# Taking the causal mask of the row maxima from TensorE to VectorE, and putting the first memory-attention units ahead of the last projections

## The chip, the cores and the metric

The kernel runs on one core of a Trainium2 chip, as one program. The metric is the device time of one execution in microseconds (us). TensorE (PE in the profile, with its weight loads as PEld), VectorE (DVE), ScalarE (ACT) and GpSimd (POOL) each run their own queue of instructions in order; SyncE (SP) issues most transfers.

## The reference, cut to what matters

Two decoder layers over 2,048 positions of width 1,024. Each has 12 heads of causal softmax attention (layer 0 with low-rank projections and a rotary part, layer 1 with a forget-gate bias) and 4 heads of attention over 256 memory tokens, fed by one combined input projection and followed by gating, an output projection and a norm.

```python
def causal_block_attention(q, k, v, scale, log_f_cum=None):
    ...
        s = jnp.einsum('bqhd,bkhd->bhqk', q_i, k, preferred_element_type=jnp.float32) * scale
        if log_f_cum is not None:
            s = s + (args[2][..., None].astype(jnp.float32) - f_t[:, :, None, :].astype(jnp.float32))
        q_pos = i * BLOCK_Q + jnp.arange(BLOCK_Q)
        mask = key_pos[None, :] <= q_pos[:, None]
        s = jnp.where(mask, s, -jnp.inf)
        p = jax.nn.softmax(s, axis=-1)
        return jnp.einsum('bhqk,bkhd->bqhd', p.astype(v.dtype), v)

def memory_attention(q, k, v):
    s = jnp.einsum('bshd,bmhd->bhsm', q, k, preferred_element_type=jnp.float32) * (MEM_DIM ** -0.5)
    p = jax.nn.softmax(s, axis=-1)
    return jnp.einsum('bhsm,bmhd->bshd', p.astype(v.dtype), v)
```

## The kernel before, in words

The program goes through input projection, attention and output projection of layer 0, then the same of layer 1. A number of full precision is held as a high and a low part, so that a product takes two or three matmuls.

Attention is cut into **units**: one head and one group `g` of 512 queries. A causal unit has four query tiles of 128. For each tile the **maxima** are found first: query rows against keys in chunks of up to 512 columns (L1578), each into one bank of a ring of three PSUM banks (`ap["pm"]`), and VectorE reduces each chunk to one column (L1544). The last chunk of each tile is the **diagonal** one, 128, 256, 384 or 512 columns wide; its last 128 columns need the causal mask. TensorE puts it there: a matmul of the identity `idb` with the mask `mqk` (L1577) starts the bank, and the matmul of queries and keys adds to it. A unit with `g > 0` has `g + 1` chunks a tile, gathered in `mx` and reduced once more by `nm` (L1589); a unit with `g = 0` has one chunk a tile and writes the negated maximum straight to `nmw`. A small matmul then turns the four columns into a row (L1596), which VectorE writes under the queries (L1597), so that the **logits** (L1705, transposed, with a mask of their own at L1667 and L1671) come out with the maximum subtracted. ScalarE takes the exponential (L1647) and its high part (L201), GpSimd or VectorE the low part (L223), and TensorE multiplies with the **values** (L1721). A head has 4 units and 16 diagonal chunks; 24 heads have 384.

The order on all engines is written out by `run_units` under `manual_schedule`: while the logits of one unit run, the maxima of units up to `AHEAD = 5` further on are put between them. A memory unit has no mask; its maxima are at L1555.

Ahead of that, `att_start` runs the first memory units of a layer (6 in layer 0, 8 in layer 1) by `run_early`, while the last projections (L254, from `proj_b` in layer 1 and from `up_a` in layer 0) still run. Here a list scheduler sets the order by priorities, which follow the order in which the code records instructions; `high_priority(offset=n)` moves what it encloses ahead by n.

Of the kernel before, what the change touches and what calls it, by code (L numbers as in the profile page):

```python
# [10 lines left out]
F32 = mybir.dt.float32  # L11
# [10 lines left out]
P = 128  # L22
# [28 lines left out]
PV_AHEAD = 120  # L51
MEM_EARLY = {0: 6, 1: 8}
# [139 lines left out]
class Trunk:  # L192
# [64 lines left out]
    def constants(self, ctx):  # L257
# [17 lines left out]
        self.mqk = cp.tile([P, P], BF16, name="mqk")  # L275
        nc.gpsimd.memset(self.mqk, 0.0)
        nc.gpsimd.affine_select(out=self.mqk, in_=self.mqk, compare_op=ALU.is_ge, fill=NEG, base=0,
                                pattern=[[-1, P]], channel_multiplier=1)
# [738 lines left out]
    def att_start(self, l):  # L1017
# [27 lines left out]
        run_early(mem, first)  # L1045
# [30 lines left out]
    def attention(self):  # L1076
# [6 lines left out]
        gb, fewer = B("G"), None  # L1083
        more = (v0, yb, gb, ap["sp"]) if l == 0 else (ap["ymp"], gb, v0, v0)
# [401 lines left out]
class Unit:  # L1486
# [46 lines left out]
    def max_closures(self):  # L1533
# [11 lines left out]
        if not self.causal:  # L1545
# [13 lines left out]
            self.nchunk = 1  # L1559
            return out  # L1560
        self.nchunk = g + 1
        for t in range(4):
            nk = (4 * g + t + 1) * P
            for c in range(self.nchunk):

                def f(t=t, nk=nk, c=c):
                    (q, qr), (k, kr) = self.mx_ops
                    if t == 0 and c == 0:
                        start()
                        if self.nchunk > 1:  # L1570
                            self.mx = K.sm.tile([P, 4, NG], F32, name="mx", tag="mx", bufs=AHEAD + 2)
                    x = c * G
                    w = min(G, nk - x)
                    ps = ap["pm"].tile([P, w], F32, name="pm", tag="pm")
                    diag = x + w == nk
                    if diag:
                        nc.tensor.matmul(ps[:, w - P:w], lhsT=K.idb, rhs=K.mqk, start=True, stop=False, skip_group_check=True)  # L1577
                    nc.tensor.matmul(ps, lhsT=q[0:qr, t * P:(t + 1) * P], rhs=k[0:kr, x:x + w],  # L1578
                                     start=not diag, stop=True, skip_group_check=diag)
                    if self.nchunk == 1:  # L1580
                        reduce(self.nmv[:, t:t + 1], ps, True)
                    else:
                        reduce(self.mx[:, t, c:c + 1], ps, False)
                out.append((f, min(G, nk - c * G)))
        return out

    def nm(self):
        if self.nchunk > 1:
            self.K.nc.vector.tensor_reduce(out=self.nmv, in_=self.mx[:, :, 0:self.nchunk], axis=AX.X, op=ALU.max, negate=True)  # L1589
# [201 lines left out]
```

## Time and profile before

| | |
|---|---|
| median of 3 runs | 2927.8 us (2927.29 to 2934.29) |
| the profiled execution | 2922.26 us, span of its instructions 2920.2 us |
| granted TensorE clock, mean | 0.975 |
| busy over the span | PE 2822.9 us, PEld 2394.5, DVE 1556.6, ACT 1324.8, POOL 1249.0 |
| attention of layer 0 and of layer 1 | about 650 to 1290 us, 2170 to 2705 us |

Busy time is the time in which an engine has an instruction running. Matmuls are pipelined, and the ends that the profile gives them are modelled, so what one costs is read from start to start, not from its own duration. PEclk is the granted clock as a share of full speed: 1.00 stands for 2.4 GHz, 0.50 for 1.2 GHz.

### The profile page before, as it was taken

To read this page: it belongs to the slowest core of one execution; us is meant where nothing else is said; L and a number is where in the kernel's file an instruction comes from. 1 tells how busy PE (TensorE), PEld (TensorE's weight loads), DVE (VectorE), ACT (ScalarE), POOL (GpSimd) and SP (SyncE) were. 2 spreads that over 40 slices of the span, in tenths; PEclk is the share of its full clock that TensorE was granted. 3 is DMA by queue.
4 is the path that set the end of the run, shared out by engine and by line. 5 is a ranking of instruction groups with operands and counts; after the bars stand their busy time and mean duration, and the time that the engine had idled before them with its cause. 6 is when DMAs were issued, how large, how long until landed. Compare 5 with 4: busy or idle time off the path is not lost. (4 is left out here: it accounts for less than half of the span.)

```text
span 2920.2 us, 58773 instructions
## 1 busy us (share of the span) xinstructions
PE 2822.9 (97%) x24401; PEld 2394.5 (82%) x24401; DVE 1556.6 (53%) x2950; ACT 1324.8 (45%) x1867; POOL 1249.0 (43%) x836
## 2 busy tenths in 40 slices
PE   7999999879999999999999999999999999999998
PEld 6789998657788888878888988999767788787787
DVE  6522115567676777645463345310267687777343
ACT  5321123336777777752131010111137788888311
POOL 2110114336667777772201014200037778788421
PEclk9999999979999999999999999999979999999999
DMA  5333447763433334245443226831454444364453
GB/s 191 123 134 95 126 144 266 234 200 91 98 75 85 77 90 97 57 162 194 150 153 128 75 67 209 311 127 62 130 148 112 116 130 122 109 163 161 153 178 116
DMA packets 260931, 398.43 MB, mean 136 GB/s; under 512 B 24792, under 2 KB 140520, under 8 KB 260520
## 3 DMA queue, kind: packets, MB, share of 16 engines
q1 hardware_dynamic: 180112, 255.21, 30.8%
q10 hardware_dynamic: 79016, 138.27, 13.1%
q8 instruction: 192, 3.15, 0.5%
q0 software_dynamic: 1536, 1.18, 0.3%
q14 instruction: 75, 0.61, 0.1%
HBM read 238.13 MB, written 156.47 MB: 135 GB/s over the span
## 5 line engine op out<-in xcount | busy, mean ns | idle before, releaser
L223 POOL TENSOR_TENSOR bA<-bA,bA 128x1024 f16<-128x1024 f32 (+5 forms) x277 | 507.0, 1841 | 311.1 <-ACT bA L201 223.8
L1544 DVE TENSOR_REDUCE mx<-banks 128x1 f32<-128x512 f32 (+2 forms) x864 | 511.9, 618 | 194.2 <-PE banks L1578 188.4
L254 PE MATMUL banks<-bR,bA 128*128 128x256 f32 (+3 forms) x4437 | 551.4, 286 | 0.6 <-DVE bQ L510 0.6
L254 PEld LDWEIGHTS banks<-bR,bA 128*128 128x128 f32 x4437 | 542.9, 189 | 5.4 <-DVE bQ L510 0.8
L254 PE MATMUL banks<-bA,bR 128*128 128x512 f32 (+2 forms) x2208 | 510.1, 388 | 6.5 <-ACT bS L823 3.6
L1705 PE MATMUL banks<-bA,bA 96*128 96x512 f32 (+13 forms) x1820 | 484.1, 377 | 0.9 <-ACT bA L1647 0.8
L254 PEld LDWEIGHTS banks<-bA,bR 128*128 128x128 f32 x2208 | 401.2, 190 | 91.9 <-ACT bS L823 4.1
L1647 ACT ACTIVATE bA<-banks 128x1024 f32<-128x1024 f32 (+1 forms) x414 | 370.9, 896 | 201.2 <-PE banks L1705 177.3
L201 ACT ACTIVATE bA<-bA 128x1024 f16<-128x1024 f32 (+5 forms) x400 | 336.4, 848 | 95.1 <-DMA qrs<-bA 20.6
L1705 PEld LDWEIGHTS banks<-bA,bA 96*128 96x128 f32 (+3 forms) x1820 | 327.7, 193 | 43.4 <-ACT bA L1647 1.7
L1578 PE MATMUL banks<-bA,bA 76*128 76x512 f32 (+5 forms) x868 | 335.4, 424 | 10.0 <-DMA bA<-qbs 4.6
L208 POOL TENSOR_SCALAR bR<-bR 128x1024 fp32r<-128x1024 f32 (+3 forms) x50 | 61.6, 1231 | 403.9 <-PE banks L254 349.0
L1222 PE MATMUL banks<-bA,bA 128*128 128x512 f32 x960 | 227.5, 393 | 0.0
L1721 PEld LDWEIGHTS <-bA 128*128 128x128 f16 x5928 | 198.0, 99 | 29.7 <-issue 12.1
L1222 PEld LDWEIGHTS banks<-bA,bA 128*128 128x128 f32 x960 | 179.3, 189 | 36.3
L1705 PE MATMUL banks<-bR,bA 128*128 128x512 f32 (+6 forms) x620 | 202.3, 393 | 0.6 <-DVE bR L1597 0.3
L223 POOL TENSOR_TENSOR bR<-bR,bR 128x1024 f16<-128x1024 f32 (+2 forms) x74 | 160.0, 2162 | 89.6 <-ACT bR L201 48.0
L1193 POOL TENSOR_TENSOR bA<-bA 128x512 f32<-128x512 f32 x64 | 101.8, 1613 | 208.7 <-DMA bA<-gs 196.7
L1578 PEld LDWEIGHTS banks<-bA,bA 76*128 76x128 f32 (+1 forms) x868 | 167.4, 200 | 24.2 <-issue 9.9
L223 POOL TENSOR_TENSOR bR<-bA,bR 128x1024 f16<-128x1024 f32 (+2 forms) x76 | 154.7, 2037 | 74.1 <-ACT bR L201 28.2
L508 ACT ACTIVATE bG<-banks 128x256 f32<-128x256 f32 x128 | 49.1, 385 | 285.6 <-PE banks L254 229.2
L223 DVE TENSOR_TENSOR bR<-bR,bR 128x1024 fp32r<-128x1024 f32 (+5 forms) x66 | 79.7, 1211 | 185.6 <-POOL bR L208 169.7
(228 smaller groups left out, 3697.8 us busy)
## 6 DMA issues: line engine op xcount, KB each, us to landing
bA<-qbs SPq DMA_DIRECT2D x65, 256.0 KB
bA<-in_x_dram SPq DMA_DIRECT2D x32, 512.0 KB
gs<-bG ACTq DMA_DIRECT2D x128, 128.0 KB
bA<-gs SPq DMA_DIRECT2D x32, 512.0 KB
bA<-ys SPq DMA_DIRECT2D x32, 512.0 KB
bA<-h SPq DMA_DIRECT2D x28, 512.0 KB
ks<-bA ACTq DMA_DIRECT2D x24, 512.0 KB
qs<-bA ACTq DMA_DIRECT2D x24, 512.0 KB
```

The source lines that it names most:

```text
L201: nc.scalar.activation(out, in_, AF.Copy, scale=scale)
L208: nc.gpsimd.tensor_scalar(out, in_, scale, 0.0, op0=ALU.mult, op1=ALU.add)
L223: e.tensor_tensor(out=out, in0=in_, in1=hi, op=ALU.subtract)
L254: nc.tensor.matmul(out, lhsT=a, rhs=b, start=start and i == 0, stop=stop and i == n - 1)
L508: nc.scalar.activation(st[:, 0:2 * P], ps[:, 0:2 * P], AF.Silu)
L1193: nc.gpsimd.tensor_tensor(out=gt[:, hs], in0=gt[:, hs], in1=yt[:, hs], op=ALU.mult)
L1222: nc.tensor.matmul(ps[:, ns], lhsT=a, rhs=b[:, ns], start=c == 0 and j == 0, stop=c == KC - 1 and j == 2)
L1544: nc.vector.tensor_reduce(out=to, in_=ps, axis=AX.X, op=ALU.max, negate=negate)
L1578: nc.tensor.matmul(ps, lhsT=q[0:qr, t * P:(t + 1) * P], rhs=k[0:kr, x:x + w], start=not diag, stop=True, skip_group_check=diag)
L1647: nc.scalar.activation(pf[:, 0:w], ps[:, 0:w], AF.Exp, scale=self.scale, bias=LOGP)
L1705: nc.tensor.matmul(ps[:, o:o + bw], lhsT=k[0:kr, (self.k0 + kt) * P:(self.k0 + kt + 1) * P], rhs=q[0:qr, q0:q0 + bw], start=i == 0 and not ...
L1721: nc.tensor.matmul(self.pv[:, t, 0:n], lhsT=p[:, o:o + P], rhs=v[:, kv, a:a + n], start=self.first, stop=False, skip_group_check=True)
```

## The change

The mask of the maxima leaves TensorE. `tensor_tensor_reduce` on VectorE takes the bank and the mask, adds them, writes the sum to a scratch tile `mj` and the maximum to `mx`. The mask tile is now 512 wide, zero but for its last 128 columns, and made on GpSimd at the start of each layer's attention. A unit with `g = 0` goes by `mx` and `nm` like the others. Beside it, `run_early` is enclosed in a priority offset of 1500.

```diff
+EARLY_AHEAD = 1500
...
-        self.mqk = cp.tile([P, P], BF16, name="mqk")
-        nc.gpsimd.memset(self.mqk, 0.0)
-        nc.gpsimd.affine_select(out=self.mqk, in_=self.mqk, compare_op=ALU.is_ge, fill=NEG, base=0,
-                                pattern=[[-1, P]], channel_multiplier=1)
...
-        run_early(mem, first)
+        with self.tc.high_priority(offset=EARLY_AHEAD):
+            run_early(mem, first)
...
+        mb, jb = (v0, yb) if l == 0 else (ap["sp"],) * 2
+        mqk = self.mqk = mb.tile([P, G], BF16, name="mqk")
+        ap["mj"] = Turn(jb.tile([P, G], BF16, name="mj"))
+        nc.gpsimd.memset(mqk, 0.0)
+        nc.gpsimd.affine_select(out=mqk[:, G - P:G], in_=mqk[:, G - P:G], compare_op=ALU.is_ge, fill=NEG, base=0,
+                                pattern=[[-1, P]], channel_multiplier=1)
...
-                    diag = x + w == nk
-                    if diag:
-                        nc.tensor.matmul(ps[:, w - P:w], lhsT=K.idb, rhs=K.mqk, start=True, stop=False, skip_group_check=True)
-                    nc.tensor.matmul(ps, lhsT=q[0:qr, t * P:(t + 1) * P], rhs=k[0:kr, x:x + w],
-                                     start=not diag, stop=True, skip_group_check=diag)
-                    if self.nchunk == 1:
-                        reduce(self.nmv[:, t:t + 1], ps, True)
+                    nc.tensor.matmul(ps, lhsT=q[0:qr, t * P:(t + 1) * P], rhs=k[0:kr, x:x + w], start=True, stop=True)
+                    to = self.mx[:, t, c:c + 1]
+                    if x + w == nk:
+                        nc.vector.tensor_tensor_reduce(out=ap["mj"].next()[:, 0:w], in0=ps, in1=K.mqk[:, G - w:G], scale=1.0,
+                                                       scalar=-3.0e38, op0=ALU.add, op1=ALU.max, accum_out=to)
                     else:
-                        reduce(self.mx[:, t, c:c + 1], ps, False)
+                        reduce(to, ps, False)
...
     def nm(self):
-        if self.nchunk > 1:
-            self.K.nc.vector.tensor_reduce(out=self.nmv, in_=self.mx[:, :, 0:self.nchunk], axis=AX.X, op=ALU.max, negate=True)
+        if not self.causal:
+            return
+        self.K.nc.vector.tensor_reduce(out=self.nmv, in_=self.mx[:, :, 0:self.nchunk], axis=AX.X, op=ALU.max, negate=True)
```

The first causal unit of layer 0 on TensorE, before: four masks, each with a weight load of its own, and the four diagonal chunks behind them, ahead of the row matmul.

```order
L1577 LDWEIGHTS idb
L1577 MATMUL banks<-mqk,idb 128x128
L1578 MATMUL banks<-bA_5120,bA_5290 128x128
L1577 LDWEIGHTS idb
L1577 MATMUL banks<-mqk,idb 128x128
L1578 MATMUL banks<-bA_5120,bA_5290 128x256
L1577 LDWEIGHTS idb
L1577 MATMUL banks<-mqk,idb 128x128
L1578 MATMUL banks<-bA_5120,bA_5290 128x384
```

The same place on TensorE in the changed kernel, where the chunks have line 1577 and the row matmul line 1597:

```order
L1597 MATMUL banks<-idr,nmw 68x128
L1577 MATMUL banks<-bA_5115,bA_5289 128x128
L1577 MATMUL banks<-bA_5115,bA_5289 128x256
L1577 MATMUL banks<-bA_5115,bA_5289 128x384
L1577 MATMUL banks<-bA_5115,bA_5289 128x512
L1597 MATMUL banks<-idr,nmw 68x128
```

The masks and their weight loads are gone, 384 of each in the program; nothing else on TensorE has moved here. On VectorE the same unit was four reduces in a row, between two writes of rows under queries:

```order
L1597 TENSOR_TENSOR bA_4690<-banks,spread 4x512
L1544 TENSOR_REDUCE nmw<-banks 128x1 x4
L1597 TENSOR_TENSOR bA_4690<-banks,spread 4x512
L1544 TENSOR_REDUCE mx<-banks 128x1 x3
L1597 TENSOR_TENSOR bA_5290<-banks,spread 4x512
```

In the changed kernel (`bA_5267` holds the scratch tile, `bA_5114` the mask):

```order
L1580 ISA bA_5267,mx<-banks,bA_5114 128x128
L1580 ISA mx 128x1
L1580 ISA bA_5267,mx<-banks,bA_5114 128x256
L1580 ISA mx 128x1
L1580 ISA bA_5267,mx<-banks,bA_5114 128x384
L1580 ISA mx 128x1
L1580 ISA bA_5267,mx<-banks,bA_5114 128x512
L1580 ISA mx 128x1
L1598 TENSOR_TENSOR bA_4685<-banks,spread 4x512
L1590 TENSOR_REDUCE nmw<-mx 128x4
```

Each diagonal chunk is now two instructions, the sum with its maximum and a second one that writes the [128, 1] result; behind the four stands one more reduce. The program has 768 such instructions in place of 384 reduces, and 96 reduces at `nm` in place of 72.

TensorE at the end of the projections of layer 1, before: the last nine projection matmuls (L254), with maxima and logits of memory units around them.

```order
L1555 MATMUL banks<-bA_21294,bR_21298 128x256 x2
L1705 MATMUL banks<-bA_21294 128x512 x2
L254 MATMUL banks<-bA_14744,bR_16184 128x512
L254 MATMUL banks<-bA_14745,bR_16184 128x512
L254 MATMUL banks<-bA_14744,bR_16185 128x512
L1555 MATMUL banks<-bA_21294 128x256 x2
L1705 MATMUL banks<-bR_21298,bA_21294 128x512
L1596 MATMUL banks<-idr,nmw 68x128
```

In the changed kernel (projections at L255, maxima of memory units at L1559, logits at L1706):

```order
L1559 MATMUL banks<-bA_21125,bR_21129 128x256 x2
L1706 MATMUL banks<-bR_21129,bA_21125 128x512 x2
L255 MATMUL banks<-bA_14575,bR_16016 128x512
L255 MATMUL banks<-bA_14575,bR_16015 128x512
L255 MATMUL banks<-bA_14576,bR_16015 128x512
L255 MATMUL banks<-bA_14575,bR_16016 128x512
L1559 MATMUL banks<-bA_21125 128x256 x2
L1706 MATMUL banks<-bR_21129,bA_21125 128x512
L1597 MATMUL banks<-idr,nmw 68x128
```

The rows read alike but belong to the unit after: 239 projection matmuls stand behind the first memory unit's first maxima, where there were 192, and the values of six of the eight early units stand ahead of the last projection, where there were five. In layer 0 the order of the early units among the projections is the same, row by row, on all engines.

## Rows read from the trace of the kernel before

**Rows 1.** The page, busy time, share of the span and instructions of each engine.
```profile
PE 2822.9 (97%) x24401; PEld 2394.5 (82%) x24401; DVE 1556.6 (53%) x2950; ACT 1324.8 (45%) x1867; POOL 1249.0 (43%) x836
```
**Rows 2.** Busy time by stretch: start:end, length, busy us (instructions) of each engine, PEclk, DMA.
```profile
876.00:949.00 73.00, 72.98 (x878) 59.69 (x874) 50.85 (x91) 57.06 (x72) 54.26 (x31) 1.00 0.34 85
...
2409.00:2482.00 73.00, 72.70 (x1000) 59.15 (x996) 57.52 (x103) 63.18 (x72) 60.28 (x29) 1.00 0.47 121
```
**Rows 3.** Groups by line: count, busy us, mean ns, idle before and what ended it.
```profile
L1544 DVE TENSOR_REDUCE mx<-banks 128x1 f32<-128x512 f32 (+2 forms) x864 | 511.9, 618 | 194.2 <-PE banks L1578 188.4
...
L1577 PE MATMUL banks<-mqk,idb 128*128 128x128 bf16 x384 | 88.8, 233 | 1.1 <-DVE mx L1544 0.5
...
L1596 PE MATMUL banks<-idr,nmw 128*68 128x128 f32 (+1 forms) x128 | 32.2, 251 | 7.0 <-DVE nmw L1544 5.6 <-DVE bA L1597 1.1 <-DVE nmw L1589 0.3
```
**Rows 4.** TensorE in order of time, layer 0: start us, us, what.
```profile
1004.07 0.40 PE L1578 MATMUL banks<-bA,bR 96*128 96x512 f32 x1
1004.30 1.63 PE L1721 MATMUL banks<-bA,bR 128*128 128x65 f16 x48
1005.77 0.22 PE L1577 MATMUL banks<-mqk,idb 128*128 128x128 bf16 x1
1005.80 0.48 PE L1578 MATMUL banks<-bA,bR 96*128 96x512 f32 x1
1006.12 1.57 PE L1705 MATMUL banks<-bR,bA 100*128 100x512 f32 x6
1007.52 0.23 PE L1577 MATMUL banks<-mqk,idb 128*128 128x128 bf16 x1
1007.56 0.31 PE L1578 MATMUL banks<-bA,bA 96*128 96x128 f32 x1
1007.71 0.23 PE L1577 MATMUL banks<-mqk,idb 128*128 128x128 bf16 x1
```
**Rows 5.** Groups by line and form, VectorE in the attention of layer 0.
```profile
L1544 DVE TENSOR_REDUCE mx<-banks 128x1 f32<-128x512 f32 x322 | 218.5, 685 | 93.0 <-PE banks L1578 90.9
L1597 DVE TENSOR_TENSOR bA<-banks,spread 4x512 fp32r<-4x512 f32 x43 | 29.9, 696 | 10.1 <-PE banks L1596 9.3
...
L1589 DVE TENSOR_REDUCE nmw<-mx 128x4 fp32r<-128x12 f32 x12 | 2.0, 166 | 0.4
```
**Rows 6.** A write of [128, 1] without input on VectorE, least/median/most ns.
```profile
L292 DVE MEMSET vmax<- x4: 59/59/59, 0.9 to 1.0; 128x1 f32 x4
```
**Rows 7.** Groups by line: ScalarE's read of its accumulator.
```profile
L1233 ACT ACTIVATION_READ_ACCUMULATOR bA<-banks 128x1 f32 x31 | 6.0, 193 | 0.0
```
**Rows 8.** VectorE in order of time: two reduces of 512 columns back to back.
```profile
2186.07 1.28 DVE L1544 TENSOR_REDUCE mx<-banks 128x1 f32<-128x512 f32 x2
```
**Rows 9.** Busy time by stretch: two of a head in layer 0, two in layer 1.
```profile
1007.91:1020.29 12.38, 12.38 (x137) 9.92 (x137) 11.23 (x21) 10.18 (x14) 7.70 (x4) 1.00 0.13 32
1020.29:1035.38 15.09, 15.09 (x213) 12.63 (x211) 9.04 (x17) 12.26 (x15) 12.58 (x7) 1.00 0.21 71
2480.66:2492.13 11.47, 11.18 (x150) 8.86 (x150) 9.62 (x19) 9.19 (x11) 8.70 (x6) 1.00 0.38 103
2492.13:2504.18 12.05, 12.05 (x181) 9.95 (x177) 8.54 (x16) 10.76 (x11) 11.27 (x6) 1.00 0.21 65
```
**Rows 10.** TensorE in order of time, layer 1: last projections, first mask.
```profile
2147.14 2.27 PE L254 MATMUL banks<-bA,bR 128*128 128x512 f32 x9
...
2170.09 0.33 PE L1577 MATMUL banks<-mqk,idb 128*128 128x128 bf16 x1
```
**Rows 11.** Busy time by stretch, between those two.
```profile
2149.40:2170.10 20.70, 17.87 (x111) 12.15 (x111) 20.04 (x32) 6.96 (x9) 10.47 (x13) 0.57 0.51 143
```
**Rows 12.** Busy time by stretch where the granted clock falls and comes back, layer 1.
```profile
2148.00:2152.00 4.00, 3.18 (x14) 1.81 (x12) 2.69 (x3) 1.84 (x3) 1.97 (x2) 1.00 0.57 164
2152.00:2156.00 4.00, 3.42 (x29) 2.39 (x29) 3.91 (x8) 0.76 (x2) 1.38 (x3) 0.55 0.12 45
2152.00:2196.00 44.00, 41.72 (x227) 29.54 (x228) 35.45 (x64) 16.29 (x19) 18.55 (x16) 0.50 0.48 128
2192.00:2196.00 4.00, 4.00 (x21) 2.89 (x21) 2.42 (x6) 1.60 (x3) 0.92 (x1) 0.50 0.45 104
2196.00:2200.00 4.00, 4.00 (x55) 3.13 (x52) 3.15 (x9) 2.71 (x4) 2.14 (x1) 0.90 0.46 127
```
**Rows 13.** Busy time by stretch: the same passage of layer 0.
```profile
584.00:657.00 73.00, 57.40 (x330) 42.68 (x328) 47.67 (x85) 26.57 (x43) 27.00 (x24) 0.72 0.64 200
```
**Rows 14.** The mask's making on GpSimd, least/median/most ns.
```profile
L277 POOL TENSOR_SCALAR_AFFINE_SELECT mqk<-mqk x1: 369/369/369, 1.9 to 1.9; 128x128 bf16<-128x128 bf16 x1
```

More of the change, by code (lines that the diff above doesn't have):

```diff
@@ L1558, in max_closures @@
                 out.append((f, G))
-            self.nchunk = 1
             return out
@@ L1569, in f @@
                         start()
-                        if self.nchunk > 1:
-                            self.mx = K.sm.tile([P, 4, NG], F32, name="mx", tag="mx", bufs=AHEAD + 2)
+                        self.mx = K.sm.tile([P, 4, NG], F32, name="mx", tag="mx", bufs=AHEAD + 2)
                     x = c * G
@@ L1587, in nm @@
     def nm(self):
-        if self.nchunk > 1:
-            self.K.nc.vector.tensor_reduce(out=self.nmv, in_=self.mx[:, :, 0:self.nchunk], axis=AX.X, op=ALU.max, negate=True)
+        if not self.causal:
+            return
+        self.K.nc.vector.tensor_reduce(out=self.nmv, in_=self.mx[:, :, 0:self.nchunk], axis=AX.X, op=ALU.max, negate=True)
     def nm_row(self):
```

## The prediction, made before the changed kernel ran

> **What bounds the kernel now.** I read the page's busy times first: TensorE is busy 97% of the span, VectorE 53%, GpSimd 43% [rows 1]. But such a share is a mean over stages, so I read the busy time by stretch inside the attention of each layer. There TensorE has no gaps at all (72.98 of 73 us, 72.70 of 73), and VectorE is the next busiest by a clear distance, 50.85 and 57.52 of 73 [rows 2]. Groups by line then say what TensorE waits for: the 384 masks (L1577) have 1.1 us of idle time ahead of them in all, the row matmuls (L1596) 7.0 us, nearly all for VectorE [rows 3]. So the attention goes at TensorE's pace, and VectorE is already the engine that it waits for when it waits. Work taken from TensorE is worth its full time until VectorE falls behind, and this change gives VectorE more to do.
>
> **What TensorE gives back.** The mean of 233 ns for a mask [rows 3] is not its price, since matmuls are pipelined. I read TensorE in order of time, from start to start. A chunk of 512 columns without a mask holds the engine for 0.23 us (1004.07 to 1004.30); with its mask ahead, 0.35 us (1005.77 to 1006.12); the difference is 0.12. A chunk of 128 with its mask takes 0.19 (1007.52 to 1007.71), of which its columns, at 0.23/512 each, are 0.06, so its mask is 0.13. The mask alone, from its start to the next, is only 0.03 to 0.04 [rows 4]; the rest shows up behind it, where the chunk waits for a weight load. I take 0.115, a little under the two differences, since a short chunk may then be held by its own weight load. 384 x 0.115 = 44.2 us. The bounds are 0.04 and 0.13: 15 and 50 us. The Trainium skill ("TensorE: Matmul & The Clock Gate", section "Back-to-back issue gap") says that a stream of weight load and matmul pairs goes at about 81 ns for 128 columns, and that an isolated matmul counts 56 ns. By 81 ns the gain would be an estimate of 31 us, and the sum below 2909 in place of 2902; the differences of 0.12 and 0.13 in this trace are above it, and I go by them.
>
> **What VectorE takes on.** Each diagonal chunk was one reduce and becomes two instructions. Call what a chunk costs more x. The first reads the bank and writes as many columns as it reads; the nearest row with a bank read, a second operand and 512 columns out is the row write, 696 ns against 685 for the reduce, so +0.011 [rows 5]. The second writes [128, 1] and appears nowhere in this trace. The floor is a write of [128, 1] without input, 0.059 [rows 6], so x is at least 0.07. The ceiling is ScalarE's read of its accumulator, 0.193 [rows 7], plus lost overlap: two reduces back to back take 1.28 where two single ones take 1.37, so 0.09 is hidden today when reduces stand in a row, and a read that needs the finished sum would not let it hide [rows 8]. That makes 0.011 + 0.193 + 0.09 = 0.30. I take 0.17, the nearest row of VectorE's own with a small [128, few] result from a small input, the reduce at `nm`, 0.166 [rows 5]. There is also one such reduce more for each head (the unit with g = 0), 0.17.
>
> **Where that meets the path.** The place where VectorE is tightest is the part of a head in which the maxima of its g = 0 and g = 1 units are found: 8 of its 16 diagonal chunks stand in one stretch of some 12 us. In layer 0 that stretch is 12.38 us with VectorE busy 11.23, in layer 1 11.47 with 9.62 [rows 9]. After the change TensorE needs 8 x 0.115 = 0.92 less, 11.46 and 10.55. VectorE needs 11.23 + 8x + 0.17 and 9.62 + 8x + 0.17. What VectorE lacks, the chunks wait for through the ring of three banks: 8x - 0.06 a head in layer 0 and 8x - 0.76 in layer 1, so at x = 0.17 a stall of 1.30 and 0.60. The stretch after it has 4 diagonal chunks and plenty of room (9.04 + 0.68 against about 14.6, 8.54 + 0.68 against about 11.6) [rows 9], so the lag is made good there and doesn't pass to the next head. I take all 12 heads of both layers as alike: 12 x 1.30 + 12 x 0.60 = 22.8 us, in general 192x - 9.8. Two errors of this stand against each other, and I let them cancel: the ring and the units worked ahead soften a lag, and not every idle moment of VectorE can be used.
>
> **The second part, and the making of the mask.** In layer 0 the order of the early units is the same on all engines: nothing, and the passage in which the clock is low there stays as it is (584 to 657). In layer 1 one of eight units moves ahead of the last projections. Between the end of the last projection (2147.14 + 2.27) and the first mask at 2170.09 lie 20.7 us [rows 10], and VectorE is busy in 20.04 of them [rows 11]: it is this work that the first causal unit waits for. A unit's VectorE work that moves ahead is at least two reduces of 0.69, a row write of 0.70, and two or three more of the same size, some 3.4 us; at most it is a third of the stretch, 6.9. I take 4 us; the bounds are 0 (VectorE is as full before the last projection) and 7. In this stretch the granted clock falls to 0.50, that is 1.2 GHz, behind 4 us in which TensorE was busy 3.18, and comes back at 2196 [rows 12]. In layer 0 it is 0.72 on average over a like passage [rows 13]. The new mask is made once a layer on GpSimd, a memset and a select of 0.37 [rows 14], in a passage where GpSimd has 27.00 us to do in 73 [rows 13]: nothing. If that cover were gone it would cost about 1 us a layer.
>
> **The sum.** Profiled execution 2922.3 - 44.2 (masks) + 22.8 (VectorE's lag) - 4 (layer 1's early unit) = 2896.9. The median of the runs shown is 5.5 above the profiled execution, so 2902 us. A measurement of this kernel can tell about 0.3%, or 8.8 us, from no change: faster is under 2919, slower over 2936.6.
>
> **The rivals.** (A) The other side: VectorE becomes the bound. If the second instruction waits for the whole sum to be written and then takes as long as ScalarE's, x is 0.30 or more; 192x - 9.8 then eats 48.2 at x = 0.302, and over 0.348 the kernel is measurably slower. At x = 0.40 it is 2922.3 - 44.2 + 67.0 - 4 + 5.5 = 2947. For it: VectorE has only 1.15 us free in the stretch of layer 0 [rows 9]. Against it: no row of VectorE shows a small instruction over 0.17. (B) The second instruction is as cheap as the memset, x = 0.07: layer 0 lags 0.50 a head, 6.0 us in all, layer 1 not at all: 2922.3 - 44.2 + 6.0 - 4 + 5.5 = 2886. (C) A mask is worth only its own 0.04, because the chunk behind it waits for a weight load that comes with or without it. Then TensorE gives 15.4, VectorE's lag is 8x - 0.66 in layer 0 alone, 8.4 us, and the time is 2917. Against it stand both differences in [rows 4]. (D) With less VectorE work behind the last projection the low clock of layer 1 goes early or never comes. The 44 us from 2152 to 2196 hold 41.72 of TensorE at half speed but also 35.45 of VectorE [rows 12], so at most some 9 us more are to be had: 2893. For it: one unit less at the place. Against: TensorE is short of work there because of VectorE, and VectorE's sum is hardly less. (E) TensorE's new short waits cost it the clock. Where it was busy 3.18 of 4 us it fell to 1.2 GHz [rows 12]. If each of 24 heads lost it for 4 us, that is 24 x 2 = 48 us, 2950. Against it: 1.3 us in 12 is a smaller share of idle time, and the stretch of layer 1 that has 0.29 us idle shows 1.00 [rows 9].
>
> **How the numbers follow.** The forecast's own case (x from 0.11 to 0.30, the masks worth 0.1 or more, the second part worth 0 to 7) has 0.47; 0.08 of that lies above 2919, where x is over 0.26. A has 0.14, of which 0.10 is beyond 2936.6; B 0.18; C 0.08, half of it within the 0.3%; D 0.08; E 0.05. Faster: 0.39 + 0.18 + 0.04 + 0.08 = 0.69. Same: 0.08 + 0.04 + 0.04 = 0.16. Slower: 0.10 + 0.05 = 0.15. The range goes down to B with D and a little more, 2868, and up into A, to 2934; what is left out is most of A's upper part and E. The forecast's own case alone is 2888 to 2927.
>
> **What would show it.** The two instructions that stand for one reduce: the pair should take 0.86 us together at 512 columns; 0.75 would be B, 1.0 and more A. TensorE from start to start at a diagonal chunk of 512 columns: 0.23 where it was 0.35 (0.31 would be C). TensorE's idle time ahead of the chunks and the row matmuls, ended by VectorE: some 23 us, at the g = 0 and g = 1 units of each head, more in layer 0, where now there are 8. VectorE in the two stretches of 73 us: some 4 to 5 us more. The granted clock in the attention: 1.00 throughout, or E. The first maxima behind the last projection of layer 1: 16 to 17 us after it, where it was 20.7, with the low clock of about the same length. The prediction is wrong if the lag is not where I put it: if VectorE falls behind in every stretch and not in the first two units of a head alone, the stall is larger than 192x - 9.8, and if the ring of three banks and the units worked ahead carry 1.3 us without a wait, it is nearly nothing and the time is 2880.

## The result, and the profile after

The changed kernel takes 2895.76 us (median of 4 runs, 2891.94 to 2904.4) against 2927.55 before: ratio 0.989, 95% interval 0.9863 to 0.9917. The forecast was 2902 with a range of 2868 to 2934. The total came out 6 us from the forecast, but its two large terms were both off, by 12 and by 18 us, and in opposite directions. Most of what follows is about that.

The profiled execution took 2891.94 us, span 2890.2, so 30.0 less in the span. The page of the changed kernel, busy time, share of the span and instructions of each engine:

```profile
PE 2787.6 (96%) x24017; PEld 2379.1 (82%) x24017; DVE 1562.0 (54%) x3358; ACT 1323.5 (46%) x1867; POOL 1249.2 (43%) x838
```

Against [rows 1], TensorE is busy 35.3 us less with 384 instructions fewer, and VectorE, with 408 instructions more, only 5.4 us more. Of these 408, 384 are the second instructions and 24 the new reduces at `nm`, which alone are worth 4. The groups of the new instructions by line and form (count, busy us, mean ns, idle before and what ended it) say why:

```profile
L1580 DVE CUSTOM_DVE_ANT_0 bA<-banks,bA 128x512 bf16<-128x512 f32 x96 | 65.8, 685 | 31.0 <-PE banks L1577 30.4
L1580 DVE CUSTOM_DVE_ANT_0 bA<-banks,bA 128x384 bf16<-128x384 f32 x96 | 53.2, 554 | 23.3 <-PE banks L1577 19.5
L1580 DVE DVE_READ_ACCUMULATOR2_ANT mx<- 128x1 f32 x384 | 31.7, 83 | 0.0
```

The sum with its maximum takes 685 ns at 512 columns, the duration of the plain reduce that it replaces [rows 5]. The second instruction takes 83 ns. In order of time (start us, us, what), the four sums of a `g = 0` unit in layer 0 of the changed kernel:

```profile
1002.39 0.29 DVE L1580 CUSTOM_DVE_ANT_0 bA<-banks,bA 128x128 bf16<-128x128 f32 x1 [0.56 <-PE banks L1577]
1002.60 0.08 DVE L1580 DVE_READ_ACCUMULATOR2_ANT mx<- 128x1 f32 x1
1002.83 0.42 DVE L1580 CUSTOM_DVE_ANT_0 bA<-banks,bA 128x256 bf16<-128x256 f32 x1
1003.18 0.08 DVE L1580 DVE_READ_ACCUMULATOR2_ANT mx<- 128x1 f32 x1
1003.41 0.56 DVE L1580 CUSTOM_DVE_ANT_0 bA<-banks,bA 128x384 bf16<-128x384 f32 x1
1003.89 0.08 DVE L1580 DVE_READ_ACCUMULATOR2_ANT mx<- 128x1 f32 x1
1003.89 0.18 DVE L1730 RECIPROCAL r<-banks 128x4 f32<-128x4 f32 x1
```

The second instruction starts 0.08 us before the first has ended (1002.60 against 1002.39 + 0.29), and the reciprocal at the end starts together with the last of them. So the pair holds VectorE no longer than the first instruction alone. Only where one sum follows another is there a hole, 0.15 us, from 1002.68 to 1002.83 and from 1003.26 to 1003.41. The same three chunks before, on VectorE:

```profile
1007.91 1.13 DVE L1544 TENSOR_REDUCE nmw<-banks 128x1 fp32r<-128x128 f32 x3 [0.70 <-PE banks L1578]
```

1.13 us there, 1.58 now (1002.39 to 1003.97): the two holes and the overlap lost with them, 0.22 each.

TensorE in order of time at the same place. Before, the three masked chunks begin at 1007.52 [rows 4] and end with the start of the values:

```profile
1008.26 0.39 PE L1721 MATMUL banks<-bA,bR 128*128 128x65 f16 x7
```

After, the same three chunks and the values behind them:

```profile
1002.13 0.56 PE L1577 MATMUL banks<-bA,bA 96*128 96x128 f32 x3
1002.53 0.66 PE L1722 MATMUL banks<-bA,bR 128*128 128x65 f16 x16
```

Three masked chunks took 0.74 us, three without masks 0.40: 0.113 a mask, as forecast. But now the masked chunk of 512 columns from which the forecast took its 0.12, the one at 1005.77 in [rows 4]. In the changed kernel the same chunk of the same unit stands ahead of the same six logits:

```profile
1000.40 0.48 PE L1577 MATMUL banks<-bA,bR 96*128 96x512 f32 x1
1000.72 1.57 PE L1706 MATMUL banks<-bR,bA 100*128 100x512 f32 x6
```

It takes 0.32 without its mask, where it took 0.35 with it. The mask gave back 0.03 here, not 0.12; by the sign that the prediction set for this row (0.23 forecast, 0.31 for rival C) this one chunk speaks for C. The 0.23 that I compared it with belonged to a chunk ahead of values. Taking all 354 diagonal chunks at which neither trace has a wait, from start to the start of what follows, before less after, the mean is 0.091 us: 0.12 where another chunk follows, about 0.07 for a chunk of 128 ahead of values, 0.03 for most of those of 512 columns ahead of logits or the row matmul.

Busy time by stretch, over the part of a head with the maxima of its `g = 0` and `g = 1` units, this time cut at TensorE's first chunk of the one and of the unit after. Before, one head of each layer:

```profile
1007.56:1019.89 12.33, 12.33 (x134) 10.11 (x134) 10.87 (x20) 9.97 (x13) 8.05 (x4) 1.00 0.12 32
2396.84:2407.56 10.72, 10.44 (x125) 8.35 (x124) 8.69 (x17) 8.45 (x11) 8.91 (x5) 1.00 0.43 122
```

The same two in the changed kernel:

```profile
1002.13:1014.04 11.91, 11.66 (x127) 9.71 (x125) 10.56 (x28) 9.82 (x13) 8.11 (x4) 1.00 0.12 31
2374.93:2385.28 10.35, 9.92 (x116) 7.96 (x115) 8.68 (x25) 8.37 (x11) 9.02 (x5) 1.00 0.51 140
```

TensorE is busy 0.67 and 0.52 us less for eight masks, 0.084 and 0.065 each, and idle 0.25 us where it had been idle for none in layer 0, 0.43 where it had been 0.28 in layer 1. VectorE's busy time has not risen in either. These are heads out of the last eight of their layer, whose stretches are nearly alike in the changed kernel (called regular below). In each of them the stretch has one wait of TensorE over 0.1 us, and what ends it is the row write under the queries. The row matmul takes a bank of the ring of three as well, and the row write (L1598) frees it. In the head of layer 0 above:

```profile
1005.98 0.50 PE L1577 MATMUL banks<-bA,bA 96*128 96x512 f32 x1 [0.24 <-DVE bR L1598]
```

TensorE's idle time by line:

```profile
L1577 PE MATMUL banks<-bA,bA 76*128 76x512 f32 (+5 forms) x868 | 316.9, 406 | 16.7 <-DVE bA L1598 4.9 <-DMA bA<-qbs 3.7 <-DMA bA<-qrs 3.2
L1597 PE MATMUL banks<-idr,nmw 128*68 128x128 f32 (+1 forms) x128 | 31.9, 249 | 3.6 <-DVE nmw L1548 2.8 <-DVE nmw L1590 0.4
```

Before, the chunks' line was:

```profile
L1578 PE MATMUL banks<-bA,bA 76*128 76x512 f32 (+5 forms) x868 | 335.4, 424 | 10.0 <-DMA bA<-qbs 4.6 <-DMA bA<-qrs 2.4 <-DVE bA L1597 2.0
```

The chunks waited 10.0 us before and wait 16.7 now, the masks 1.1 and none, the row matmuls 7.0 [rows 3] and 3.6: some 2 to 3 us more in all, where 15 more were forecast (23 against 8). The two stretches of 73 us answer to [rows 2] (not at the same heads, since the time has moved):

```profile
876.00:949.00 73.00, 72.79 (x886) 60.62 (x885) 52.50 (x116) 58.49 (x74) 57.24 (x33) 1.00 0.36 90
2390.00:2463.00 73.00, 72.09 (x973) 58.96 (x972) 60.75 (x137) 63.78 (x72) 61.69 (x30) 1.00 0.46 122
```

TensorE has gaps of 0.21 and 0.91 us, where it had 0.02 and 0.30, VectorE 1.7 and 3.2 us more of work, where 4 to 5 were forecast, and the granted clock is 1.00. It is not 1.00 in all of the attention, before or after: in the stretch of the third head of layer 0 and of the third and fourth of layer 1 it is 0.89, 0.88 and 0.88 before, 0.81, 1.00 and 0.88 after (0.50 in the first head of each layer, before and after). So such falls are not new with the change. In layer 1 the first chunk comes at 2152.64, 13.5 us after the last four projections (2138.05 + 1.10), where it was 20.7 [rows 10]:

```profile
2138.05 1.10 PE L255 MATMUL banks<-bA,bR 128*128 128x512 f32 x4
2152.64 0.47 PE L1577 MATMUL banks<-bA,bA 76*128 76x128 f32 x1 [0.57 <-DVE nmw L1548]
```

The low clock is still there, and somewhat shorter: 0.50 from 2142 to 2178 and back to 1.00 behind 2182, some 37 us where it was 44 [rows 12]:

```profile
2138.00:2142.00 4.00, 3.12 (x13) 1.81 (x13) 3.36 (x6) 2.63 (x4) 1.57 (x2) 1.00 0.54 148
2142.00:2178.00 36.00, 34.24 (x173) 24.36 (x172) 30.05 (x66) 13.46 (x15) 16.94 (x15) 0.50 0.53 137
2178.00:2182.00 4.00, 4.00 (x54) 3.20 (x53) 2.69 (x7) 2.70 (x3) 1.52 (x1) 0.80 0.26 79
```

### The profile page after: what moved, and what is told of

Read it like the earlier page. It is cut to its first block, busy times and chain, and to the rows that moved or that the text cites. A ratio compares the mean times of both kernels' runs of the same rounds, so it can differ in the third digit from the quotient of the medians.

```text
span 2890.2 us, 58604 instructions
## 1 busy us (share of the span) xinstructions
PE 2787.6 (96%) x24017; PEld 2379.1 (82%) x24017; DVE 1562.0 (54%) x3358; ACT 1323.5 (46%) x1867; POOL 1249.2 (43%) x838
## 5 line engine op out<-in xcount | busy, mean ns | idle before, releaser
L255 PE MATMUL banks<-bR,bA 128*128 128x256 f32 (+3 forms) x4437 | 553.3, 287 | 0.6 <-DVE bQ L507 0.6
L255 PEld LDWEIGHTS banks<-bR,bA 128*128 128x128 f32 x4437 | 544.6, 190 | 5.6 <-DVE bQ L507 0.8
L255 PE MATMUL banks<-bA,bR 128*128 128x512 f32 (+2 forms) x2208 | 510.9, 388 | 6.4 <-ACT bS L820 3.6
L1706 PE MATMUL banks<-bA,bA 96*128 96x512 f32 (+13 forms) x1820 | 483.4, 377 | 0.7 <-ACT bA L1648 0.6
L255 PEld LDWEIGHTS banks<-bA,bR 128*128 128x128 f32 x2208 | 400.5, 190 | 92.1 <-ACT bS L820 4.4
L1548 DVE TENSOR_REDUCE mx<-banks 128x1 f32<-128x512 f32 x576 | 388.2, 686 | 107.5 <-PE banks L1577 104.7
L1706 PEld LDWEIGHTS banks<-bA,bA 96*128 96x128 f32 (+3 forms) x1820 | 327.3, 193 | 43.3 <-ACT bA L1648 1.3
L1577 PE MATMUL banks<-bA,bA 76*128 76x512 f32 (+5 forms) x868 | 316.9, 406 | 16.7 <-DVE bA L1598 4.9
L1580 DVE CUSTOM_DVE_ANT_0 bA<-banks,bA 128x128 bf16<-128x128 f32 (+3 forms) x384 | 186.9, 487 | 77.3 <-PE banks L1577 66.4
L1706 PE MATMUL banks<-bR,bA 128*128 128x512 f32 (+6 forms) x620 | 201.3, 390 | 0.9 <-DVE bR L1598 0.9
```

The source lines that it names most:

```text
L255: nc.tensor.matmul(out, lhsT=a, rhs=b, start=start and i == 0, stop=stop and i == n - 1)
L1548: nc.vector.tensor_reduce(out=to, in_=ps, axis=AX.X, op=ALU.max, negate=negate)
L1580: nc.vector.tensor_tensor_reduce(out=ap["mj"].next()[:, 0:w], in0=ps, in1=K.mqk[:, G - w:G], scale=1.0, scalar=-3.0e38, op0=ALU.add, op1=A ...
L1706: nc.tensor.matmul(ps[:, o:o + bw], lhsT=k[0:kr, (self.k0 + kt) * P:(self.k0 + kt + 1) * P], rhs=q[0:qr, q0:q0 + bw], start=i == 0 and not ...
```

## The experiments

Eleven kernels ran in three groups, each group beside the kernel before on one chip. The median of the latter was 2929.3 us beside the first four, 2929.82 beside the next four and 2928.01 beside the last three.

**The second part alone.** The kernel before, with

```diff
-        run_early(mem, first)
+        with self.tc.high_priority(offset=EARLY_AHEAD):
+            run_early(mem, first)
```

> The second part alone: the masks stay on TensorE, the early memory units have their offset of 1500. Both theories: 0 in layer 0, 4 to 7 us less in layer 1, so 2921 to 2924 against 2927.5 before. Rival, that it moves nothing (VectorE as full before the last projection as behind it): 2927 or 2928. The profile of the changed kernel shows 21.2 us between the last projection of layer 1 and the first maxima shrink to 13.8; if that is the second part and not the masks, it shows here too.

2924.93 us, ratio 0.9987, interval 0.9977 to 0.9997: 4 us less, by the interval 1 to 7. The stretch between the last projections and the first mask has become 15.4 us (the last four projections at 2158.81 + 1.10, the first mask at 2175.33), so it is this part that shortens it:

```profile
2158.81 1.10 PE L255 MATMUL banks<-bA,bR 128*128 128x512 f32 x4
2175.33 0.27 PE L1579 MATMUL banks<-mqk,idb 128*128 128x128 bf16 x1 [2.50 <-DVE nmw L1546]
```

Part of it is given back ahead of it, where the unit's matmuls now stand among the projections: from the first matmul of the projections' line behind the attention of layer 0 to the last it takes 673.6 us (1486.27 to 2159.91), and in the kernel before 670.3 (1479.12 to 2149.41).

**The first part alone.** The changed kernel without the offset.

```diff
-        with self.tc.high_priority(offset=EARLY_AHEAD):
-            run_early(mem, first)
+        run_early(mem, first)
```

> The first part alone: masks on VectorE, no offset for the early units. Theory 1, the prediction's terms (44 us from TensorE, 23 us given back to VectorE's lag): 21 us less than before, about 2906. Theory 2 (a mask is worth about 0.08 us, and the ring and the units worked ahead absorb nearly all of VectorE's lag, 3 to 5 us left): 27 to 29 us less, about 2900.

2901.05 us, ratio 0.9896 (0.9883 to 0.991): 28 us less by the medians, 26 to 34 by the interval. That is theory 2. The two parts add up: 4 and 28 are 32, as measured for both.

**No mask at all.**

```diff
-                    if x + w == nk:
-                        nc.vector.tensor_tensor_reduce(out=ap["mj"].next()[:, 0:w], in0=ps, in1=K.mqk[:, G - w:G], scale=1.0,
-                                                       scalar=-3.0e38, op0=ALU.add, op1=ALU.max, accum_out=to)
-                    else:
-                        reduce(to, ps, False)
+                    reduce(to, ps, False)
...
-        nc.vector.reciprocal(r, self.pv[:, :, DH])
+        nc.vector.tensor_scalar(r, self.pv[:, :, DH], 1.0e-30, None, op0=ALU.max)
+        nc.vector.reciprocal(r, r)
```

> The mask of the maxima is left out altogether: a diagonal chunk has neither the mask matmul nor the sum on VectorE, only the plain reduce as before, so the maxima also run over later keys, and the sums of the exponentials are held above 1e-30 by one small instruction more before the reciprocal. What it gains over the changed kernel (2895.8) is what VectorE's lag costs there. Theory 1: 23 us, so 2873. Theory 2: 3 to 5 us, so 2891 to 2893.

This kernel leaves the causal mask out of the maxima. 2899.35 us, ratio 0.9893 (0.988 to 0.9907): no faster than the changed kernel. Theory 1's 23 us are not there, nor anything of their size. The run can't tell 0 from the 3 to 5 us of theory 2, since its own small instruction ahead of each reciprocal stands on VectorE in the same stretch (the layer 0 stretch takes 11.85 us, with 0.19 of TensorE's idle time left). The run with two scratch tiles, below, does tell it.

**Each mask twice on TensorE**, in the kernel before:

```diff
                         nc.tensor.matmul(ps[:, w - P:w], lhsT=K.idb, rhs=K.mqk, start=True, stop=False, skip_group_check=True)
+                        nc.tensor.matmul(ps[:, w - P:w], lhsT=K.idb, rhs=K.mqk, start=False, stop=False, skip_group_check=True)
```

> The kernel before with each mask of the maxima put twice on TensorE (384 matmuls and weight loads more, and no word more for VectorE): the price of one mask measured by itself. Theory 1, 0.115 us each: 44 us more, 2971. Theory 2, about 0.08: 31 us more, 2959. Rival C of the prediction, 0.04: 15 us more, 2943.

2944.43 us, ratio 1.0042 (1.0028 to 1.0056): 15 us more by the medians, 8 to 16 by the interval, 0.02 to 0.04 a mask. By itself that speaks for rival C, and both theories missed. But a second mask behind a first need not be priced like the first: its stationary operand is the one just used, though the trace has a weight load for each of the two. The next two runs price the first.

**Both masks**, in the changed kernel; and the same with **one column** of zeros:

```diff
-                    nc.tensor.matmul(ps, lhsT=q[0:qr, t * P:(t + 1) * P], rhs=k[0:kr, x:x + w], start=True, stop=True)
+                    diag = x + w == nk
+                    if diag:
+                        nc.tensor.matmul(ps[:, w - P:w], lhsT=K.idb, rhs=K.mqk[:, G - P:G], start=True, stop=False, skip_group_check=True)
+                    nc.tensor.matmul(ps, lhsT=q[0:qr, t * P:(t + 1) * P], rhs=k[0:kr, x:x + w],
+                                     start=not diag, stop=True, skip_group_check=diag)
```
```diff
-                        nc.tensor.matmul(ps[:, w - P:w], lhsT=K.idb, rhs=K.mqk[:, G - P:G], start=True, stop=False, skip_group_check=True)
+                        nc.tensor.matmul(ps[:, w - P:w - P + 1], lhsT=K.idb, rhs=K.mqk[:, 0:1], start=True, stop=False, skip_group_check=True)
```

> The changed kernel with the mask put on TensorE as well (128 columns of identity times mask at the start of each diagonal bank; the sum on VectorE stays, and adds it a second time). It prices the first mask of a chunk in the changed kernel. If the price is what the regular heads of the two traces show, 0.083 to 0.091 us: 32 to 35 us slower than the changed kernel, 2928 to 2931. If it is the 0.035 that a second mask cost in the run with each mask twice: 13 us, 2910. If the prediction's 0.115: 44 us, 2941.

> As the run with both masks, but the matmul on TensorE has one column of zeros in place of 128 of the mask: the instruction and its weight load stay, the columns go. If the weight load and the wait of the next one for it are most of a first mask's price (0.083 less 0.035 for the columns): 17 to 21 us slower than the changed kernel, 2913 to 2917. If the columns are the price: 2896 to 2900. If the matmul's columns hide under the weight load altogether: as with 128, about 2929.

Both masks: 2924.39 us, ratio 0.9982 (0.9968 to 0.9995). In the stretch of layer 0, TensorE's busy time goes back from 11.66 to the 12.32 us of before, 0.083 a mask, 31.9 us for 384:

```profile
1011.84:1024.16 12.32, 12.32 (x134) 10.11 (x134) 11.04 (x28) 9.94 (x13) 8.02 (x4) 1.00 0.13 32
```

The kernel takes 26.7 us more than the changed kernel run again (2897.74, below, in another group), 26 by the two ratios, 0.070 a mask; that is net of the idle time that TensorE loses again with the masks back (none in the 12.32). So a first mask costs about 0.083 us (0.065 to 0.091 by the readings so far), neither 0.115 nor 0.04. One column: 2925.01 us, ratio 0.9993 (0.9979 to 1.0007), not to be told from 128 columns. So the price is not that of the columns. What it does consist of stays open: the second mask of the run before has a weight load of its own too, and costs at most half.

The kernel with both masks holds a second answer. Its TensorE does all that it did before and its VectorE all that it does after the change, with the offset for the early units; it takes 2924.39 us where the offset alone took 2924.93. At TensorE's pace of before, the sum on VectorE costs nothing that can be measured.

**The sum twice on VectorE**, in the changed kernel: the call stands there two times, with the same operands.

```diff
                         nc.vector.tensor_tensor_reduce(out=ap["mj"].next()[:, 0:w], in0=ps, in1=K.mqk[:, G - w:G], scale=1.0,
                                                        scalar=-3.0e38, op0=ALU.add, op1=ALU.max, accum_out=to)
+                        nc.vector.tensor_tensor_reduce(out=ap["mj"].next()[:, 0:w], in0=ps, in1=K.mqk[:, G - w:G], scale=1.0,
+                                                       scalar=-3.0e38, op0=ALU.add, op1=ALU.max, accum_out=to)
```

> The changed kernel with the sum and maximum of each diagonal chunk taken twice on VectorE, a bit over 0.6 us more a chunk (0.40 for the instructions, 0.23 where one such sum follows another). Theory 1, the prediction's stall by stretch: the first two units of a head hold 8 such chunks, 5 us more, where VectorE has 1.3 to 1.7 free: 3.3 to 3.7 a head, about 84 us, 2980. Theory 2, the lag is spread over the whole head (units worked ahead): layer 0 has room for 10 us a head, layer 1 lacks 3 to 4: about 40 us, 2936. If VectorE is never near the bound: under 5 us.

3006.0 us, ratio 1.0255 (1.0238 to 1.0272): 108 us over the changed kernel. Theory 2 (the lag spreads over the head) is out, and theory 1's way of reckoning, stretch by stretch, holds, though 24 us short. Busy time by stretch in this kernel: the stretch of layer 0, the rest of that head, and the stretch of layer 1:

```profile
1038.56:1056.07 17.51, 15.49 (x127) 12.50 (x125) 16.45 (x45) 9.81 (x13) 8.08 (x4) 0.81 0.09 23
1056.07:1092.58 36.51, 36.51 (x460) 30.32 (x459) 28.76 (x69) 30.04 (x40) 31.92 (x21) 1.00 0.47 116
2455.12:2469.69 14.57, 12.19 (x116) 9.49 (x115) 12.12 (x42) 8.35 (x11) 8.99 (x5) 0.88 0.47 123
```

The stretch of the next head of layer 0 in the same kernel:

```profile
1092.58:1108.07 15.49, 12.81 (x127) 9.77 (x125) 14.73 (x43) 10.18 (x13) 8.12 (x4) 1.00 0.29 69
```

VectorE is now the bound of the stretch, 16.45 of 17.51 us, and TensorE is idle for 2.02; the rest of the head, the second row, has TensorE without a gap, so nothing is made good there. And rival E appears: in the first and third row, with 2.0 and 2.4 us of idle time, the granted clock is 0.81 and 0.88 (a mean over time at 2.4 and at 1.2 GHz), and TensorE is busy for 15.49 us with what took it 11.66. In the next head it is 1.00, and there the stretch takes 15.49 us, 3.6 more than in the changed kernel: theory 1's 3.3 to 3.7. Of the eight regular heads of layer 0 three are like that one; the other five have a clock of 0.80 or 0.81 and take 17.4 to 17.7 us. So the fallen clock costs each of the five some 2 us, and at least a part of the 24 us that theory 1 lacks is the clock's. In layer 1 all eight regular heads have 0.79 to 0.88, and its part there can't be told.

**Two banks in place of three** in the ring of the maxima:

```diff
-        ap["pm"], ap["ps"], ap["pv"] = self.banks(1, 2, 3), BankRing(self.psum, 4, 4), self.banks(0)
+        ap["pm"], ap["ps"], ap["pv"] = self.banks(1, 2), BankRing(self.psum, 4, 4), self.banks(0)
```

> The changed kernel with two banks in place of three in the ring of the maxima in the attention. If it is the ring that lets VectorE's sums lie beside TensorE's work, a chunk then waits for the reduce of two chunks ahead and the time is well over 10 us up; if the order (logits and values between the maxima) alone gives the room, under 5 us.

3006.74 us, ratio 1.0258 (1.0243 to 1.0273): 109 us over the changed kernel, with VectorE's work untouched. TensorE's idle time ahead of the chunks:

```profile
L1577 PE MATMUL banks<-bA,bA 76*128 76x512 f32 (+5 forms) x868 | 346.2, 425 | 58.5 <-DVE mx L1548 42.0 <-DVE bA L1598 6.2 <-DVE mx L1580 4.1
```

So it is the third bank that lets VectorE's work as a whole lie beside TensorE's. For the sums by themselves the run says less: 42.0 us of these waits are for plain reduces (L1548) and 4.1 for sums (L1580), and most of the loss lies outside the tight stretch. In a head of layer 0 the stretch takes 13.06 us (11.91 in the changed kernel) and the rest of the head 38.76 (36.27). The kernel before with two banks was not run.

**The changed kernel again, and with two scratch tiles.** In the second, the four sums in a row write two tiles by turns:

```diff
-        ap["mj"] = Turn(jb.tile([P, G], BF16, name="mj"))
+        ap["mj"] = [jb.tile([P, n], BF16, name=f"mj{n}") for n in (G, G - P)]
...
-                        nc.vector.tensor_tensor_reduce(out=ap["mj"].next()[:, 0:w], in0=ps, in1=K.mqk[:, G - w:G], scale=1.0,
+                        nc.vector.tensor_tensor_reduce(out=ap["mj"][w // P % 2][:, 0:w], in0=ps, in1=K.mqk[:, G - w:G], scale=1.0,
```

> The changed kernel itself once more, so that the runs beside it have it on the same chip: 2894 to 2900, 1.0 to 1.2% below the kernel before.

> The changed kernel with two scratch tiles for the sums, used by turns, in place of one. In the trace a sum that follows another on VectorE starts 0.144 us after the other's second instruction, and only then. If that is the wait for the one scratch tile, the pair of 128 and 256 columns goes from 0.44 us start to start to about 0.21, the cost beside other instructions. On the time: leaving out the sum altogether shortened the first two units of a head by 0.05 us, so at most 1 to 2 us off, not to be told from the changed kernel. If VectorE's lag were on the path (the prediction's theory), 3 x 0.23 us a head: 16 us off.

Again: 2897.74 us, ratio 0.9893 (0.9878 to 0.9908). Two scratch tiles: 2897.4 us, ratio 0.9889 (0.9874 to 0.9903), not to be told from it, as expected. But the trace tells: the three sums in a row on VectorE,

```profile
999.17 0.29 DVE L1580 CUSTOM_DVE_ANT_0 bA<-banks,bA 128x128 bf16<-128x128 f32 x1 [0.56 <-PE banks L1577]
999.38 0.08 DVE L1580 DVE_READ_ACCUMULATOR2_ANT mx<- 128x1 f32 x1
999.38 0.42 DVE L1580 CUSTOM_DVE_ANT_0 bA<-banks,bA 128x256 bf16<-128x256 f32 x1
...
1000.21 0.08 DVE L1580 DVE_READ_ACCUMULATOR2_ANT mx<- 128x1 f32 x1
```

have no hole and take 1.12 us (999.17 to 1000.29), as the three reduces did before (1.13). The hole was the wait of a sum for the scratch tile of the one before it. And the stretch of layer 0:

```profile
998.91:1010.58 11.67, 11.66 (x126) 9.71 (x125) 10.58 (x28) 9.81 (x13) 8.13 (x4) 1.00 0.13 31
```

It is 11.67 us, with TensorE's idle time gone, where the changed kernel has 11.91: VectorE's lag in a regular head of layer 0 was 0.24 us and came from these holes alone. In layer 1 the stretch shrinks by as much in seven of the eight regular heads, which take 10.33 to 10.42 us in the changed kernel and 10.09 to 10.17 here; in the eighth, the head of layer 1 shown before, it stays at 10.33. One of the seven, in the changed kernel and with two tiles:

```profile
2415.62:2425.99 10.37, 9.91 (x116) 7.93 (x115) 8.71 (x25) 8.37 (x11) 9.00 (x5) 1.00 0.59 158
2421.60:2431.69 10.09, 9.70 (x116) 7.93 (x115) 8.57 (x25) 8.36 (x11) 8.98 (x5) 1.00 0.60 159
```

Fifteen such heads are some 4 us, which the medians (0.3 us apart, each run's times 8 to 9 us apart) don't show.

**The mask behind the chunk**, in the kernel before: the diagonal chunk starts the bank and the mask adds to it.

```diff
-                    if diag:
-                        nc.tensor.matmul(ps[:, w - P:w], lhsT=K.idb, rhs=K.mqk, start=True, stop=False, skip_group_check=True)
                     nc.tensor.matmul(ps, lhsT=q[0:qr, t * P:(t + 1) * P], rhs=k[0:kr, x:x + w],
-                                     start=not diag, stop=True, skip_group_check=diag)
+                                     start=True, stop=not diag, skip_group_check=diag)
+                    if diag:
+                        nc.tensor.matmul(ps[:, w - P:w], lhsT=K.idb, rhs=K.mqk, start=False, stop=True, skip_group_check=True)
```

> The kernel before with the mask matmul behind the diagonal chunk in place of ahead of it: as many instructions, columns and weight loads, in another order. If a mask's price is that the weight load of the next matmul finds only a short matmul to lie under, the load that is uncovered is now that of whatever follows the chunk (values and logits among them, whose price in the table by successor would then fall away or move): between 15 us faster and 15 slower than before. If the price is the two instructions in themselves, nothing changes: 2925 to 2931. In either case no change of VectorE's work.

2927.34 us, ratio 0.9996 (0.9985 to 1.0008): no change. Where the mask stands beside its chunk doesn't matter, that it is there does. Whether the price is a weight load that isn't covered, and which one, was not settled by it.

## Why the prediction came out right, and where its steps failed

**What bounds the kernel** was read rightly: TensorE's time came back as time of the kernel (35.3 us less busy, 30.0 less span), and VectorE was what TensorE waited for in the regular heads when it waited.

**The masks' price failed.** "I take 0.115, a little under the two differences" gave 44.2 us. Measured with the mask put back: 0.083, 32 us (27 by the whole runs, net of idle time, and 35 by the mean over the chunks). The mistake was to difference two chunks that stand ahead of different instructions, and to take two places for all. At the place itself the chunk without its mask takes 0.32, not 0.23. The estimate that stood beside it from the Trainium skill ("TensorE: Matmul & The Clock Gate", section "Back-to-back issue gap"), 81 ns for a weight load and matmul of 128 columns in a stream, or 31 us, was the better one, and the runs agree with it (0.083); they don't with its 56 ns for an isolated matmul. The agreement is one of size: one column cost as much as 128, and a second such pair behind the first 0.02 to 0.04 us. Rival C (0.04) is out for the first mask of a chunk, and right for a second.

**VectorE's extra failed too.** x was taken as 0.17 between 0.07 and 0.30. The trace shows no single x: next to nothing where another kind of instruction follows, since the second instruction lies under the end of the first, and 0.22 where a sum follows a sum, which is a wait for the scratch tile that the forecast did not see. In the unit shown, that is two of the four chunks; in the whole program it is 54 of the 384 sums. So the floor of 0.07, a second instruction that takes its whole time for itself, was no floor, and rival B's x was nearer than the forecast's.

**The stall** was forecast as 22.8 us and is about 5: 0.25 us a head in layer 0 and 0.15 in layer 1 (0.43 less 0.28), times 12 each. That takes all heads for regular ones. Summed over the stretches of all 24 heads, TensorE's idle time rises from 11.0 to 12.6 us, by 1.6 only, since the kernel before had single waits of its own (0.86 and 1.05 us in two heads of layer 0). The way of the wait was the forecast's, the ring of three banks: in the regular heads a chunk waits for the bank that a row matmul took before it; the row write (L1598) frees it, and this stands behind the sums on VectorE and comes later by their holes. In layer 1 the kernel before had the same wait, 0.28 us for L1597; the two scratch tiles took 0.24 off the stretch in either layer. The reckoning by stretch, 8x - 0.06, held with more work (the sum twice: 3.6 us where the clock stayed, and nothing made good later in the head), but not at this size. With two holes of 0.22 for 8x and 0.083 a mask it gives 0.12 us in layer 0 and none in layer 1, since the wait arises at one place and VectorE's free time elsewhere in the stretch doesn't undo it. And the forecast fed it with too large an x and too large a gain of TensorE: at 0.083 a mask TensorE's part of the stretch is 0.26 us longer than I had it, and this is room for VectorE.

**The second part** was forecast as 4 us and measured as 4 (1 to 7). The stretch ahead of the first chunk fell by more than forecast (to 13.5 us, and to 15.4 in the changed kernel run again, not 16 to 17), and some 3 us of that are given back among the projections. The low clock of layer 1, rival D, became shorter by some 7 us without going; how much of the 4 us that is was not separated. In layer 0 the order was the same, and the passage reads much alike (584 to 657 us: TensorE busy for 57.40 us at a clock of 0.72 before, 55.46 at 0.76 after).

**The sum**, put right by what was measured: 32 from the masks less 5 of VectorE's lag, plus 4 from the early unit, is 31 us, against 30 (the changed kernel again) and 32 measured. The forecast's terms, 44.2 less 22.8 plus 4, made 25.4. That the total came so near is luck: its two wrong terms, 12 and 18 us too large, pulled against each other.

**Rivals A and E** were real mechanisms but a good way off: the kernel with the sum twice shows both at once, at some 0.6 us more a chunk.

## What to carry to other kernels

The price of a short matmul between long ones is not its columns (one cost as much as 128 here) and not its difference to some other chunk: compare at the same successor, or put back the one that was taken out and time it. One more behind the first is no measure of the first (0.02 to 0.04 us against 0.083). An instruction whose result is written by a second one need not cost more than the first, but a scratch output that nobody reads can make each wait for the one before; two tiles ended that here (0.24 us a head, too little for the medians to show). Before moving work to an engine that has room on average, take the one stretch in which it has least, and ask what buffer lets it lag there.

## What was not expected of the hardware

- The sum and maximum of two operands takes VectorE 685 ns at 512 columns, as the plain reduce does; the read of its accumulator takes 83 ns and lies under the end of the first (it starts 0.08 us before the first ends), so the pair costs VectorE no more than the first alone.
- A second matmul with the same stationary operand right behind the first costs 0.02 to 0.04 us, at most half of the first's 0.083, with a weight load of its own in the trace. A matmul of one column costs as much as one of 128 (2925.01 and 2924.39 us).
- The same stretch in the kernel with the sum twice had a mean granted clock of 0.80 or 0.81 in five regular heads of layer 0, with 1.8 to 2.4 us of idle time of TensorE, and of 1.00 in the other three, with 2.7. So the idle time of the stretch alone doesn't tell where the clock falls.
